# The product with v in two float32r halves, and an order of all instructions computed in the kernel

## The chip, the cores and the metric

The kernel runs on one core of a Trainium2 chip. The metric is the device time of one execution in microseconds (us), the median of several runs.

## The reference

Two requests (512 and 256 tokens, width 1024) go through the same two layers, in float32. Of a layer only the shape matters here; the change sits in the attentions, the three branches a, b and d:

```
h = rms_norm(x) * (1 + scale) + shift            # adaLN: scale, shift, gate from c
z = h @ w_in                                     # split into 14 parts
oa = MLA(4 heads, v of 64 columns)
ob = differential attention(4 heads, two softmaxes each, v of 64 columns)
oc = bidirectional RG-LRU
od = GQA(4 heads, 2 key heads, q and k normalised, v of 64 columns)
o  = concat(oa * silu(ga), ob * silu(gb), oc * silu(gc), od * silu(gd))
x  = x + gate * (o @ w_out)
```

An attention head is `p = softmax(q k^T * scale); o = p @ v`, over all keys of its own request.

## The kernel before, in words

**Numbers.** Most products run in float32r: each operand is split into a high part (rounded to float32r, written by ScalarE) and a low part (the rest, subtracted on VectorE or GpSimd), and `mm3` (L280 to L283) issues three matmuls, high by high, high by low, low by high. Where an operand is left in float32, one matmul does it; the profile shows such a matmul as two records on PE.

**Tokens.** Group 0 is the request of 512 tokens (four tiles of 128), group 1 the one of 256 (two tiles).

**An attention head** goes through three steps. The scores (L761 for b, L701 and L702 for d, `mm3` for a) go to PSUM buffers `s`, of which there are two. VectorE takes the extremes (L518, L520), ScalarE the exponential with its sum. In `transpose_pv` (L525) P is transposed tile by tile on PE (L535) into PSUM buffers `tr`, of which there are three, and copied to SBUF as `pt` by `copy(EN_E[...])`: key tiles 0, 1 and 3 of a head by ScalarE (L115), tile 2 by VectorE (L194). Then L542 multiplies v (float32, 64 columns) with P^T (float32, 512 or 256 columns). Even key tiles go to columns 0 to 63 of the array, odd ones to columns 64 to 127, so that two products can stand side by side; `o_evac` (L549) adds the two halves of the result. Over the 24 heads of the two layers and both groups that makes 96 products of 512 columns and 48 of 256. v comes from a projection as [tokens, 64 columns a head], copied by ScalarE in `v_evac` (L611), in tiles made by `v_tiles` (L604).

**What fills the gaps.** The other work of a layer (projections of the next branch, gates, adaLN chunks of 8 float32 matmuls with 32 columns at L227, weight splits) is written in between the heads' steps by `weave`, in a number per step that constants set (`F_D`, `F_A`, `F_B`, `LAG_*`). The recording layer's own scheduler then decides in what order the instructions stand on each engine. Buffers are named by a tag: `b` (47 of [128, 512]), `pt` (6), `p` (6), and so on. DMAs are issued by SP's queue in order; in branch b the stacks of q and k are put together by small DMAs (L747, L749).

**Stages of a layer**, with their times in the profiled execution for the first layer: projections to 92 us, branches d and a with the projections of a in between from 92 to 265, the LRU and the projections of b to 322, branch b to 437, the output projection after that. The second layer repeats them.

Of the kernel before, what the change touches and what calls it, by code (L numbers as in the profile page):

```python
# [18 lines left out]
P = 128  # L19
D = 1024  # L20
KC = 8
# [7 lines left out]
# order of the branches' chunks in the output projection  # L29
# [7 lines left out]
# steps of other work per job of a branch, by layer  # L37
# [6 lines left out]
# engines in turn: v DVE, g Pool, a ACT  # L44
# [8 lines left out]
EN_E, EN_V = ("aav", "a")  # L53
# [21 lines left out]
def body(ctx, tc, I, O, dbg=None):  # L75
# [5 lines left out]
    BUFS = {"ws": 4, "wh": 6, "wl": 6, "b": 47, "p": 6, "pt": 6, "rot": 2, "tmp": 2, "t1": 4}  # L81
# [19 lines left out]
    def gt(g, box, dt=F32R):  # L101
        """a [128, tokens of the group] tile; two of the small group share a slot, the second of them waiting in box"""
# [17 lines left out]
    # ---------------------------------------------------------------- constants  # L120
# [14 lines left out]
    # silu(c) in columns 0, 1 of a 32-column tile of the array, the others zero  # L135
# [13 lines left out]
    # rows 0..3 are rewritten, the others stay zero  # L149
# [5 lines left out]
    def rsqrt(v, n, tag="rs_y", bufs=3):  # L155
        """v ** -0.5 for a small tile [128, n]"""
# [58 lines left out]
    # ---------------------------------------------------------------- adaLN  # L215
# [5 lines left out]
    def ada_chunk(l, j, evac, deep):  # L221
        """512 columns: row 32 j + group is the partial sum over the chunks k = j (mod 4), in a column tile of its own"""
# [29 lines left out]
    def ada_gate(l):  # L252
        """gate rows of the two groups, to DRAM"""
# [15 lines left out]
    def load_split(src, n, kg, ncol, tl="wl", th="wh", eng="g"):  # L269
        """granules of kg contraction chunks x ncol columns, split into hi and lo"""  # L270
# [1033 lines left out]
```

## Time and profile before

| | |
|---|---|
| median of 3 runs | 966.57 us (966.34 to 968.16) |
| profiled execution | span 972.5 us; no time of its own is given beside the span |
| PE busy | 916.4 us |
| VectorE (DVE) busy | 667.2 us |
| ScalarE (ACT) busy | 546.6 us |
| GpSimd (POOL) busy | 148.8 us |
| granted TensorE clock, mean | 0.98 |

A busy PE is not PE at its peak: a matmul's record runs from its start to its modelled end, and the next one starts before that. The time that a matmul takes from the others is the step from its start to the start of the next, which the timeline shows.

### The profile page before, as it was taken

The numbers are of one execution on the slowest core, as the hardware profiler recorded it, in microseconds if no ns is written. First come the engines' busy times: TensorE is split into PE (matmuls) and PEld (weight loads), VectorE is DVE, ScalarE is ACT, GpSimd is POOL, SyncE is SP. The second block draws the span as 40 slices with busy tenths as digits, with TensorE's granted clock in tenths as the row PEclk, the third lists the DMA queues.
The fourth block names the chain that finished last, engine by engine and source line by source line (L and its number), as shares of the span: only waits on it lengthen the run. The fifth ranks groups of instructions, "written<-read, shape, count | busy, mean of one in ns | idle before, by whom it ended". The sixth has DMA issues, their size and how long they took to land.

```text
span 972.5 us, 15324 instructions
## 1 busy us (share of the span) xinstructions
PE 916.4 (94%) x5248; PEld 698.9 (72%) x5248; DVE 667.2 (69%) x1714; ACT 546.6 (56%) x1331; POOL 148.8 (15%) x168
## 2 busy tenths in 40 slices
PE   4899999999999799999999989999999899999996
PEld 1598767667989465676888976665689888666785
DVE  5687876655497656678556897676456786877745
ACT  4543878756545435466346367788447445667512
POOL 0221002003120010033202111000041212010610
PEclk9899999999999799999999999999999999999998
DMA  9731012123202633446611111020331114324502
GB/s 337 244 96 55 1 55 77 33 87 87 66 22 73 184 104 105 154 129 216 214 54 44 44 55 66 1 66 11 109 109 44 65 58 115 83 71 132 173 24 107
DMA packets 54350, 91.71 MB, mean 94 GB/s; under 512 B 9072, under 2 KB 13936, under 8 KB 54272
## 3 DMA queue, kind: packets, MB, share of 16 engines
q1 hardware_dynamic: 54272, 90.73, 30.1%
q8 instruction: 42, 0.69, 0.3%
q14 instruction: 36, 0.29, 0.1%
HBM read 73.38 MB, written 6.31 MB: 82 GB/s over the span
## 4 chain that ended last, share of the span: by engine, by line
PE 72%; DVE 13%; DMA 6%; issue 3%; ACT 3%; SPq 2%; POOL 1%; DVEq 0%; POOLq 0%; ACTq 0%
PE acc L281 10%; PE acc L283 10%; PE pv L542 10%; PE acc L282 9%; PE tr L535 5%; PE tr L281 4%; PE tr L282 3%; PE tr L283 3%; PE s L281 3%; PE s L282 3%; PE s L283 3%; DMA b<-ada 2%; PE acc L227 2%; PE tr L619 2%; PE s L761 2%
## 5 line engine op out<-in xcount | busy, mean ns | idle before, releaser
L212 POOL TENSOR_TENSOR wl<-ws,wh 128x512 fp32r<-128x512 f32 (+3 forms) x56 | 74.5, 1334 | 418.6 <-ACT wh L115 315.6
L115 ACT ACTIVATE p<-s,mx 128x512 f32<-128x512 f32 (+1 forms) x192 | 117.1, 615 | 30.6 <-DVE mx L518 27.5
L281 PE MATMUL acc<-wh,b 128*128 128x256 f32 (+4 forms) x360 | 113.0, 314 | 2.6 <-DVE rs_t L163 1.6
L282 PE MATMUL acc<-wl,b 128*128 128x256 f32 (+4 forms) x360 | 111.6, 310 | 0.0
L283 PE MATMUL acc<-wh,b 128*128 128x256 f32 (+4 forms) x360 | 111.2, 310 | 0.3 <-POOL b L318 0.3
L518 DVE TENSOR_REDUCE mx<-s 128x1 f32<-128x512 f32 x128 | 86.7, 686 | 27.8 <-PE s L761 17.6
L281 PE MATMUL acc<-b,wh 128*128 128x512 f32 (+1 forms) x288 | 103.3, 359 | 1.4 <-ACT wh L115 1.4
L542 PE MATMUL pv<-pt,b 128*64 128x512 f32 (+1 forms) x288 | 102.9, 546 | 1.4 <-ACT pt L115 1.0
L283 PE MATMUL acc<-b,wl 128*128 128x512 f32 (+1 forms) x288 | 102.0, 354 | 0.0
L282 PE MATMUL acc<-b,wh 128*128 128x512 f32 (+1 forms) x288 | 100.9, 350 | 0.0
L115 ACT ACTIVATE wh<-ws 128x512 fp32r<-128x512 f32 (+3 forms) x100 | 63.3, 639 | 41.4 <-PE tr L283 13.6
L535 PEld LDWEIGHTS tr<-c,p 128*128 128x128 f32 x480 | 55.2, 141 | 34.5 <-issue 17.9
L535 PE MATMUL tr<-c,p 128*128 128x128 f32 x480 | 75.9, 278 | 4.1 <-DVE b L864 2.2
L115 ACT ACTIVATE pt<-tr 128x512 f32<-128x512 f32 (+1 forms) x120 | 58.2, 511 | 35.2 <-PE tr L535 34.7
L281 PEld LDWEIGHTS acc<-wh,b 128*128 128x128 f32 (+1 forms) x360 | 68.8, 191 | 9.6 <-issue 2.4
L283 PEld LDWEIGHTS acc<-wh,b 128*128 128x128 f32 (+1 forms) x360 | 68.5, 191 | 6.9 <-issue 5.2
L282 PEld LDWEIGHTS acc<-wl,b 128*128 128x128 f32 (+1 forms) x360 | 69.2, 192 | 2.4 <-issue 0.8
L281 PEld LDWEIGHTS acc<-b,wh 128*128 128x128 f32 x288 | 55.0, 191 | 15.2 <-issue 5.2
L283 PEld LDWEIGHTS acc<-b,wl 128*128 128x128 f32 x288 | 54.8, 190 | 14.5 <-issue 7.8
L283 PE MATMUL tr<-wh,b 128*128 128x256 f32 (+2 forms) x216 | 62.1, 287 | 0.0
L281 PE MATMUL tr<-wh,b 128*128 128x256 f32 (+2 forms) x216 | 62.1, 287 | 0.0
L282 PE MATMUL tr<-wl,b 128*128 128x256 f32 (+2 forms) x216 | 62.0, 287 | 0.0
(306 smaller groups left out, 2201.5 us busy)
## 6 DMA issues: line engine op xcount, KB each, us to landing
ws<-wf SPq DMA_DIRECT2D x40, 256.0 KB, 3.2
b<-ada SPq DMA_DIRECT2D x32, 256.0 KB, 5.4
ws<-wt SPq DMA_DIRECT2D x32, 256.0 KB, 2.9
wh<-ada SPq DMA_DIRECT2D x32, 256.0 KB, 4.5
wl<-ada SPq DMA_DIRECT2D x32, 256.0 KB, 3.6
ws<-wo SPq DMA_DIRECT2D x32, 256.0 KB, 3.3
b<-b SPq DMA_DIRECT2D x112, 64.0 KB, 2.0
b<-b SPq DMA_DIRECT2D x112, 32.0 KB, 1.9
```

Source lines behind the costliest of these rows:

```text
L115: return nc.scalar.activation(out, in_, f, **kw)
L212: engine(eng).tensor_tensor(lo, w, hi.bitcast(F32), op=ALU.subtract)
L227: nc.tensor.matmul(acc[c:c + 32], cs[:, k], w, start=(k < 4), stop=(k >= 4))
L281: nc.tensor.matmul(out, sh, mh, start=first, stop=False)
L282: nc.tensor.matmul(out, sh, ml, start=False, stop=False)
L283: nc.tensor.matmul(out, sl, mh, start=False, stop=last)
L518: V.tensor_reduce(mx[:, i:i + 1], views[i], axis=AX.X, op=ALU.min)
L535: nc.tensor.transpose(tr[:, qt * P:(qt + 1) * P], Ps[qt // 2][:, qt % 2, kt * P:(kt + 1) * P], ident)
L542: nc.tensor.matmul(pv[64 * i:64 * i + 64, :n], vt[g][:, k0 + i], pts[i][:, :n], start=(k0 == 0), stop=(k0 + 2 == nk))
L619: nc.tensor.transpose(tr[:rows, i * P:(i + 1) * P], src(tt), ident)
L761: lambda out, qt: nc.tensor.matmul(out, q[:96, qt * P:(qt + 1) * P], k[:96], start=True, stop=True), g, h2, d) for (q, k), d in
```

## The change

It does four things.

1. **The product with v.** v is split into a high and a low float32r part, which lie side by side as 128 columns of the array: columns 0 to 63 high, 64 to 127 low. P^T is split too, by `split_evac`: ScalarE writes the high part, VectorE subtracts to get the low one. Each key tile now has two float32r matmuls, P^T low first and then P^T high, both over all 128 columns, so that the sum of the two halves that `o_evac` makes holds all four products. `EN_E` and `EN_V`, which chose the copying engine, are gone. The v tiles are twice as large.
2. **The order of products.** `mm3` issues the high by high product last instead of first, and the two-product scores of branch d the low keys first.
3. **The order of all instructions.** After the kernel is recorded, `arrange` goes through all of its instructions. It works out which depends on which, gives each a duration, and lists them as they would come ready: at each step the instruction that can start first on its engine, at equal times the one written first, with buffers handed out in the order in which the code asks for them. The list is then laid on the program as one chain of order without waits. The constants of `weave` stay.
4. **Buffers.** `b` has 51 instead of 47, `pt` 9 instead of 6; a smaller scratch area for DMA descriptors frees the room.

```diff
-    BUFS = {"ws": 4, "wh": 6, "wl": 6, "b": 47, "p": 6, "pt": 6, "rot": 2, "tmp": 2, "t1": 4}
+    BUFS = {"ws": 4, "wh": 6, "wl": 6, "b": 51, "p": 6, "pt": 9, "rot": 2, "tmp": 2, "t1": 4}
...
-    def mm3(out, sh, sl, mh, ml, first, last):
-        nc.tensor.matmul(out, sh, mh, start=first, stop=False)
-        nc.tensor.matmul(out, sh, ml, start=False, stop=False)
-        nc.tensor.matmul(out, sl, mh, start=False, stop=last)
+    def mm3(out, sh, sl, mh, ml, first, last, fresh="m"):
+
+        prods = [(sh, ml), (sl, mh), (sh, mh)]
+        if fresh == "s":
+            prods[:2] = prods[1::-1]
+        for i, (s, m) in enumerate(prods):
+            nc.tensor.matmul(out, s, m, start=first and i == 0, stop=last and i == 2)
...
-            for k0 in range(0, nk, 2):
-                pts = []
-                for kt in (k0, k0 + 1):
-                    tr = ps("tr")
-                    for qt in range(nk):
-                        nc.tensor.transpose(tr[:, qt * P:(qt + 1) * P],
-                                            Ps[qt // 2][:, qt % 2, kt * P:(kt + 1) * P], ident)
-                    pt = sb([P, 512], tag="pt")
-                    copy(EN_E[kt % len(EN_E)], pt[:, :n], tr[:, :n])
-                    pts.append(pt)
-                # even and odd key tiles in the two column tiles of the array, side by side
-                for i in range(2):
-                    nc.tensor.matmul(pv[64 * i:64 * i + 64, :n], vt[g][:, k0 + i], pts[i][:, :n],
-                                     start=(k0 == 0), stop=(k0 + 2 == nk))
-                yield
+            for kt in range(nk):
+                tr = ps("tr")
+                for qt in range(nk):
+                    nc.tensor.transpose(tr[:, qt * P:(qt + 1) * P], Ps[qt // 2][:, qt % 2, kt * P:(kt + 1) * P], ident)
+                ph, pl = (sb([P, 512], F32R, tag="pt") for _ in range(2))
+                split_evac(ph[:, :n], pl[:, :n], tr[:, :n])
+                for i, p in enumerate((pl, ph)):
+                    nc.tensor.matmul(pv[:, :n], vt(g, kt), p[:, :n], start=(kt == 0 and i == 0),
+                                     stop=(kt == nk - 1 and i == 1))
+                if kt % 2:
+                    yield
...
-            g, i0 = (0, tt) if tt < 4 else (1, tt - 4)
             for i, vt in enumerate(both):
-                copy(EN_V[i % len(EN_V)], vt[g][:, i0], src[:, P * i:P * i + P])
+                v = vt[tt // 2][:, tt % 2]
+                split_evac(v[:, :, 0], v[:, :, 1], src[:, P * i:P * i + P].rearrange("p (h d) -> p h d", h=2))
...
+    while len(order) < n:
+        best = None
+        for e, ks in ready.items():
+            for k in ks:
+                t0 = buffers(k)
+                if t0 is None:
+                    continue
+                s = max(came[k], t0)
+                key = (max(at[e], s + REACH[e] if s else 0.0), k)
+                if best is None or key < best:
+                    best = key
...
+    for a, b in zip(order, order[1:]):
+        tc.add_manual_dep(prog[b], prog[a].name,
+                          mybir.DependencyInfo(mybir.DependencyClass.NoSync, mybir.DependencyReason.DATA), reason="order")
...
     with tile.TileContext(nc) as tc:
         body(tc, I, O)
+        arrange(tc)
```

**Place 1, PE, first layer, the first head of branch d that reaches its product with v.** L535 are the transposes of P, L542 (L539 in the change) the products with v, L701 and L702 (L704 and L705) scores of a later head, `acc` with 320 columns the projection for branch a. Before:

```order
L535 MATMUL tr_1409<-c_83,p_1183 128x128 x2
L535 MATMUL tr_1409<-c_83,p_1292 128x128 x2
L701 MATMUL s_1500<-b_1139,b_1148 128x512
L702 MATMUL s_1500<-b_1140,b_1148 128x512
L542 MATMUL pv_1401<-pt_1407,b_576 64x512
L535 MATMUL tr_1418<-c_83,p_1183 128x128
L542 MATMUL pv_1401<-pt_1414,b_576 64x512
```

Now:

```order
L285 MATMUL acc_1547<-wh_1223,b_398 128x320
L285 MATMUL acc_1547<-wl_1231,b_445 128x320
L285 MATMUL acc_1547<-wh_1229,b_446 128x320
L285 MATMUL acc_1547<-wh_1229,b_445 128x320
L704 MATMUL s_1518<-b_1147,b_1155 128x512
L705 MATMUL s_1518<-b_1146,b_1155 128x512
L539 MATMUL pv_1408<-pt_1415,b_576 128x512
L539 MATMUL pv_1408<-pt_1414,b_576 128x512
L535 MATMUL tr_1431<-c_83,p_1190 128x128
L539 MATMUL pv_1408<-pt_1426,b_576 128x512
L539 MATMUL pv_1408<-pt_1425,b_576 128x512
```

Between the transposes of the first key tile and its product stood two score matmuls; now projection matmuls (four of six shown) stand there too, and the products are two per key tile, over 128 columns. The second product still has a single transpose between it and the first.

**Place 2, PE, first layer, the start of branch b.** L761 (L764) are the scores of b, L227 (L226) a chunk of adaLN, `acc` with 512 columns a gate's projection. Before:

```order
L761 MATMUL s_3972<-b_3866,b_3865 128x512
L761 MATMUL s_3973<-b_3866,b_3865 128x512
L761 MATMUL s_3986<-b_3858,b_3857 128x512
L761 MATMUL s_3987<-b_3858,b_3857 128x512
L761 MATMUL s_3997<-b_3866,b_3865 128x512
L761 MATMUL s_3998<-b_3866,b_3865 128x512
L761 MATMUL s_4119<-b_3944,b_3943 128x512
L761 MATMUL s_4120<-b_3944,b_3943 128x512
L281 MATMUL acc_4054<-b_365,wh_4044 128x512
```

Now:

```order
L764 MATMUL s_4153<-b_4047,b_4046 128x512
L285 MATMUL acc_4235<-b_377,wh_4225 128x512
L285 MATMUL acc_4235<-b_376,wh_4225 128x512
L285 MATMUL acc_4235<-b_387,wl_4227 128x512
L764 MATMUL s_4154<-b_4047,b_4046 128x512
L285 MATMUL acc_4235<-b_388,wh_4225 128x512
L285 MATMUL acc_4235<-b_387,wh_4225 128x512
L285 MATMUL acc_4235<-b_398,wl_4227 128x512
L285 MATMUL acc_4235<-b_399,wh_4225 128x512
L764 MATMUL s_4167<-b_4039,b_4038 128x512
```

Eight scores stood in a row there, with nothing between; now three or four matmuls of a gate's projection stand between each two.

**Place 3, VectorE, the same head as in place 1.** L518 (L520) are extremes of scores, L200 scales P, rows of 128x2 belong to a norm of the projection. Before:

```order
L194 COPY pt_1423<-tr_1418 128x512
L200 TENSOR_SCALAR t_354_1373<-pt_1350,rsq_1361 128x128
L593 RECIPROCAL den_1498<-den_1498 128x2
L518 TENSOR_REDUCE mx_1513<-s_1515 128x1
L200 TENSOR_SCALAR p_1496<-p_1496,den_1498 128x512
```

Now:

```order
L460 TENSOR_TENSOR pt_1415<-tr_1409,pt_1414 128x512
L164 SCALAR_TENSOR_TENSOR rsq_1368<-rs_t_1370,rsq_1368 128x2
L162 SCALAR_TENSOR_TENSOR rs_t_1370<-rsq_1368 128x2
L460 TENSOR_TENSOR pt_1426<-tr_1420,pt_1425 128x512
L163 TENSOR_TENSOR rs_t_1370<-rs_t_1370,rs_v_1364 128x2
L591 RECIPROCAL den_1394<-den_1394 128x2
L520 TENSOR_REDUCE mx_1516<-s_1518 128x1
```

One key tile of the four was copied by VectorE (this is it); now VectorE subtracts for each of the four (two are shown), behind ScalarE's copy.

## Rows read from the trace of the kernel before

**Rows 1.** The page: span, busy time by engine, chain that ended last.

```profile
span 972.5 us, 15324 instructions
PE 916.4 (94%) x5248; PEld 698.9 (72%) x5248; DVE 667.2 (69%) x1714; ACT 546.6 (56%) x1331; POOL 148.8 (15%) x168
PE 72%; DVE 13%; DMA 6%; issue 3%; ACT 3%; SPq 2%; POOL 1%; DVEq 0%; POOLq 0%; ACTq 0%
```

**Rows 2.** Groups by form, PE: xcount | busy us, mean ns | idle before.

```profile
L542 PE MATMUL pv<-pt,b 128*64 128x512 f32 x192 | 82.6, 617 | 0.3 <-DVE pt L194 0.2
L542 PE MATMUL pv<-pt,b 128*64 128x256 f32 x96 | 20.4, 405 | 1.2 <-ACT pt L115 1.0
```

**Rows 3.** Timeline of PE around products with v: start us, us, what.

```profile
112.04 1.07 PE L542 MATMUL pv<-pt,b 128*64 128x512 f32 x2
113.04 0.33 PE L535 MATMUL tr<-c,p 128*128 128x128 f32 x1
...
124.36 1.83 PE L542 MATMUL pv<-pt,b 128*64 128x512 f32 x4
126.12 0.33 PE L535 MATMUL tr<-c,p 128*128 128x128 f32 x1
...
198.22 1.08 PE L542 MATMUL pv<-pt,b 128*64 128x512 f32 x4
199.22 0.39 PE L282 MATMUL tr<-b,kvh 128*128 128x256 f32 x1
...
229.64 0.65 PE L542 MATMUL pv<-pt,b 128*64 128x256 f32 x4
230.22 0.27 PE L237 MATMUL tr<-c,tmp 128*128 128x2 f32 x1
```

**Rows 4.** Timeline of PE in projections in float32r.

```profile
300.05 0.28 PE L281 MATMUL acc<-wh,b 128*128 128x256 f32 x1
300.17 0.28 PE L282 MATMUL acc<-wl,b 128*128 128x256 f32 x1
...
476.31 0.39 PE L281 MATMUL tr<-b,b 128*128 128x512 f32 x1
476.54 0.40 PE L282 MATMUL tr<-b,b 128*128 128x512 f32 x1
```

**Rows 5.** Groups by form, DVE and ACT, of evacuations from PSUM.

```profile
L194 DVE COPY pt<-tr 128x512 f32<-128x512 f32 x24 | 16.5, 688 | 16.9 <-PE tr L535 16.9
L458 DVE TENSOR_TENSOR b<-tr,b 128x512 fp32r<-128x512 f32 x4 | 2.7, 681 | 0.0
L458 DVE TENSOR_TENSOR b<-tr,b 128x256 fp32r<-128x256 f32 x4 | 1.6, 411 | 0.0
L639 DVE TENSOR_TENSOR t<-acc,pt 128x128 f32<-128x128 f32 x4 | 1.1, 278 | 0.0
L115 ACT ACTIVATE pt<-tr 128x512 f32<-128x512 f32 x72 | 42.0, 596 | 27.7 <-PE tr L535 27.4
```

**Rows 6.** Windows: stretch, its length, busy us of each engine, granted clock, DMA.

```profile
92.00:265.00 173.00, 172.02 (x992) 124.99 (x991) 110.32 (x294) 120.47 (x322) 22.16 (x39) 1.00 0.19 57
324.00:342.40 18.40, 13.39 (x33) 4.92 (x32) 12.66 (x22) 9.76 (x25) 1.31 (x1) 0.63 0.57 165
328.70:342.40 13.70, 9.95 (x16) 3.98 (x17) 9.32 (x16) 6.91 (x18) 1.31 (x1) 0.50 0.64 191
809.00:897.00 88.00, 85.73 (x455) 60.77 (x453) 68.57 (x146) 58.39 (x156) 7.71 (x6) 1.00 0.36 100
```

**Rows 7.** Waits of PE and its weight loads: us in total, times, longest.

```profile
PE acc L227 <- DVE rs_t L179: 13.2, 1, 13.2
PEld pv L542 <- ACT pt L115: 19.4, 45, 0.9
PEld s L761 <- ACT p L115: 13.5, 22, 1.9
PE tr L281 <- DVE rot L194: 6.0, 2, 3.0
```

More of the change, by code (lines that the diff above doesn't have):

```diff
@@ L52 @@
 EN_L = "g"
-EN_E, EN_V = ("aav", "a")
 ADA_T = ("wh", "wl") * 4
@@ L450, in feat_tile @@
                 for k in range(KC):
-                    mm3(acc[:, :n], his[k // 4][:, k % 4], los[k // 4][:, k % 4], hh[k], hl[k], k == 0, k == KC - 1)
+                    mm3(acc[:, :n], his[k // 4][:, k % 4], los[k // 4][:, k % 4], hh[k], hl[k], k == 0, k == KC - 1, "s")
                 evac(g, t0, n, acc)
@@ L700, in scores @@
                 s = q[:, qt * P:(qt + 1) * P]
-                nc.tensor.matmul(out, s, kh, start=True, stop=False)
-                nc.tensor.matmul(out, s, kl, start=False, stop=True)
+                nc.tensor.matmul(out, s, kl, start=True, stop=False)
+                nc.tensor.matmul(out, s, kh, start=False, stop=True)
             def attn():
@@ L1187, in body, with _accesses @@
         H = Hn
+def _accesses(aps):
+    for a in aps:
+        ap = getattr(a, "bass_ap", None)
+        t = getattr(ap, "tensor", None)
+        if t is None or not hasattr(t, "cap_key"):
+            continue
+        if t._space == bass.MemoryType.DRAM:
+            offs = np.array([ap.offset // 512])
+            for s, c in ap.ap:
+                offs = (offs[:, None] + s * np.arange(0, c, 1 if s >= 512 else 512) // 512).ravel()
+            p0, pn = 0, 1
+        else:
+            width = int(np.prod(t.shape[1:]))
+            p0, f0 = divmod(ap.offset, width)
+            pn = ap.ap[0][1]
+            offs = np.array([f0])
+            for s, c in ap.ap[1:]:
+                offs = (offs[:, None] + s * np.arange(c)).ravel()
+        mask = 0
+        for o in set(offs.tolist()):
+            mask |= 1 << o
+        yield t, p0, p0 + pn, mask
@@ new lines, in _cost @@
+def _cost(i):
+    kind, eng = type(i).__name__, i.engine
+    size = lambda a: int(np.prod([c for _, c in a.ap[1:]]))
+    outs = [a for a in i.outs if hasattr(a, "ap")]
+    ins = [a for a in i.ins if hasattr(a, "ap")]
+    n = max([size(a) for a in outs + ins] or [1])
+    if kind == "InstMatmult":
+        n, cols, f32 = size(i.ins[0]), size(i.ins[1]), i.ins[0].dtype == F32
+        if not f32:
+            return max(n * 0.44 + 4, 115), n / 2.4 + 172
+        if cols <= 64 and n > 128:
+            return n / 1.2 + 30, n / 0.6 + 160
+        if n == 128:
+            return 110, 273
+        return (215, 362) if n < 128 else (n / 0.6 + 8, n / 0.6 + 170)
+    if eng == mybir.EngineType.SP:
+        return (590 if outs[0].ap[0][1] == 32 else 375), n * 4 * outs[0].ap[0][1] / 230.0
+    psum = any(a.bass_ap.tensor._space == bass.MemoryType.PSUM for a in outs + ins if size(a) > 4)
+    if eng == mybir.EngineType.Activation:
+        s = 0.84 * n + (50 if psum else 92)
+        if i.func not in (AF.Copy, AF.Square):
+            s += 110
+        if len(outs) > 1:
+            s += 90
+        return s, s + 100
+    if eng == mybir.EngineType.Pool:
+        return 2.3 * n + 90, 2.3 * n + 135
+    if kind in ("InstTensorScalarPtr", "InstTensorCopy") and not psum and len([a for a in ins if size(a) == n]) == 1:
+        s = 0.66 * n + 70
+    else:
+        s = 1.04 * n + 65
+    return s, s + 80
@@ L1294 @@
     arrays = _layout(inputs)
-    nc = bacc.Bacc("TRN2", target_bir_lowering=False, num_devices=1)
+    nc = bacc.Bacc("TRN2", target_bir_lowering=False, num_devices=1, dynamic_dma_scratch_size=512)
     I = {n: nc.dram_tensor(n, a.shape, mybir.dt.from_np(a.dtype), kind="ExternalInput").ap()
```

110 lines of the change are left out of this document (107 added, 3 removed).

## The prediction

> **What bounds the kernel now.** I read the page first: PE is busy 916.4 us of a span of 972.5, VectorE 667, ScalarE 547, and 72% of the chain that ended last runs over PE [rows 1]. So time is won where PE needs fewer steps, or where it waits. Then the groups of PE by form: the products with v, 288 records of L542, are busy 82.6 + 20.4 us [rows 2]. Then the timeline around them, for the step from one start to the next, because a busy PE is not a full one: a product of 512 columns that stands alone keeps PE for 1.00 us (112.04 to 113.04); two that are issued close together take 1.00 for both; but two whose second comes late take 1.76 [rows 3]. Last the windows and waits: in branches d and a PE is busy 172 of 173 us, yet at the start of branch b it idles 5 of 18.4 us, and for 13.7 us of it the granted clock is 0.50, the 1.2 GHz level, after scores that waited for exponentials [rows 6, 7].
>
> **The products with v.** Their rows take 103.0 us of PE [rows 2]. The last record of each stretch runs 0.07 into what follows (1.07 against a step of 1.00, [rows 3]); with at most 144 stretches that is 10 at most, so PE loses 93 to 103 us to them. I take 97, since many stand in pairs. The change issues 2 x 96 float32r matmuls of 512 columns and 2 x 48 of 256, all over 128 columns. The trace shows no float32r product with v; the nearest rows are projections, which step by 0.23 us at 512 columns and 0.12 at 256 [rows 4]: 192 x 0.23 + 96 x 0.12 = 56. **Gain 41 us**, at most 47. At least 6: had all 48 pairs of 512 columns and 24 of 256 been close, they would cost 48 x 1.00 + 24 x 0.58 = 62 [rows 3].
>
> That low end is also what a rule gives. The Trainium skill, TensorEngine Tiling (Array Packing), section Tiling Modes, says under Key Properties that tiles operate independently, so that different tiles can run their matmuls in parallel. By that rule the pair was cheap already, and the sum below would end at 957 instead of 922. The close pair in this trace (1.00 us for two) agrees; the single and the staggered ones (1.00 each, 1.76 for two) show that the kernel mostly didn't get it, because the second P^T landed late: 45 waits for ScalarE's copy, 19.4 us [rows 7].
>
> **The start of branch b.** Eight scores stood in a row, each waiting for an exponential to free one of two PSUM buffers, and the order now has three or four projection matmuls between them (place 2). That work is moved from later, where PE is the bound, so what is won is PE's idle time and its slow clock. Idle: 18.4 - 13.4 = 5.0 us. The clock: 13.7 us at half speed with PE busy 9.95 [rows 6], of which full speed could save up to half, 5. **Gain 10 us.** At least 3, if the stacks' DMAs, still 24 issues in one queue, hold the scores up and the clock still falls; at most 17, where the next stretch profits too (the waits of L761 are 13.5 in all, [rows 7]).
>
> **The rest of the order.** Elsewhere the two orders stand close to each other: at the other stage borders PE still meets the same chains. The transposes of the LRU's end wait for VectorE's `rot` twice, 6.0 us, and the first matmul waits 13.2 [rows 7]; both stay. In the middle some waits for operands go. **Gain 4 us**: 56 us of PE idle in all [rows 1], less 13.2, 5 and 6 leave 32, of which I credit an eighth, as the order is much the same there; bounds 25 gained and 5 lost (an order from wrong durations makes an engine wait in line for something that is not there yet). High by high as the last product of `mm3` costs nothing in count: three steps of 0.12 or 0.23 as before [rows 4], one weight load each; but a group now starts with a low part, which lands last, so a late split stalls it one product earlier. That lies in the same bounds.
>
> **What VectorE and ScalarE pay.** VectorE subtracts the low part of 96 P^T tiles of 512 columns at 0.681, 48 of 256 at 0.411, and of 60 tiles of v at 0.278, and no longer copies 24 tiles at 0.688 [rows 5]: 65.4 + 19.7 + 16.7 - 16.5 = **+85 us**, 667 to 752. ScalarE gets 24 copies more, 24 x 0.596 = 14. No DMA is added, and GpSimd keeps its work. What hides it: PE's own work, while it has some. In d and a VectorE is busy 110 of 173 us; the share that falls there is 26 a layer (d and a: 16 x 0.681 + 8 x 0.411 - 4 x 0.688 = 11.4 each; v 3 tiles a token tile, 18 x 0.278 = 5, less what falls in the projections), so 136 of some 160: covered. In branch b of the second layer it is busy 68.6 of 88 [rows 6] and gets 11 more, while PE needs 7 less there: 80 of 81. There it is the bound, and PE's gain is mostly not to be had: 5 us. At the ends of the six branches no other work covers the last head; the product then waits for copy and subtraction in turn, one 0.68 longer: 6 x 0.68 = 4. **Cost 10 us with the borders of the projections**; below, 2 if all but the ends is covered; above, 30 if a third of the 85 shows. Three more `pt` buffers hold 4.5 key tiles in two parts each, against six tiles before; `tr` is held 0.68 longer per tile, three buffers as before. Both lie in that upper bound.
>
> **Sum.** 972.5 - 41 - 10 - 4 + 10 = 927.5 us of span. The profiled execution has no time of its own beside its span, which is 5.9 above the median of 966.6; the same 5.9 off gives **922 us**.
>
> **The rivals.**
>
> *The evacuation becomes the bound (0.16).* If VectorE can't keep up in the attentions, PE's 41 us turn into waits of L539 for VectorE, and only the order's 14 us are left: 972.5 - 14 - 5.9 = 953. For it: 80 of 81 in the second layer's branch b. Against it: 136 of 160 in d and a, and projections between transposes and products now (place 1). The Trainium skill has this as a rule, TensorEngine Tiling (Array Packing), section PSUM Bottleneck: speeding up PE doesn't speed up the evacuation of PSUM, which may become the bottleneck. No row here shows it yet.
>
> *The products gain only 6 us (0.05).* The lower end above: the new products step by 0.3 us on average instead of 0.2, as each waits for a semaphore and stands between float32 transposes. Then 972.5 - 6 - 10 - 4 + 10 - 5.9 = 957, the time of the rule on tiles too. Against it: projections with waits keep their steps [rows 4].
>
> *The order closes more (0.15).* Upper ends of the gains, 47 + 17 + 25, and 5 of cost: 972.5 - 84 - 5.9 = 883. For it: VectorE and ScalarE have 31% and 44% to spare over the span. Against it: the borders look the same in both orders.
>
> *Slower (0.06).* Each key tile's transposes need one of three `tr` buffers, which now stays taken until VectorE has subtracted. If VectorE is late, as it serves extremes of scores (0.68 each) from the same queue, PE can't transpose and can't multiply, and in order nothing behind them runs. Then the subtractions themselves, 65.4 + 19.7 = 85 us, lie on the path. The gains are 41 + 10 + 4 = 55; so the kernel gets slower once more than two thirds of the 85 show, and with all of it 972.5 - 55 + 85 - 5.9 = 997. Against it: PE's other work in d and a.
>
> *It doesn't move (0.04).* The order loses what the product wins, in waits by wrong durations: 967.
>
> **How the numbers follow.** Forecast 0.54, the rivals as given. The range takes in the forecast with its bounds, most of the better case and the evacuation bound: 885 to 953. It leaves out the slower case, no change, the 957, and a third of the better case, 0.06 + 0.04 + 0.05 + 0.05. A measurement can tell 0.2%, 1.9 us. Faster by more than that: 0.54 + 0.16 + 0.05 + 0.15 = 0.90; within it 0.04; slower 0.06.
>
> **What would show it.** Right: the products are 288 float32r matmuls that step by 0.23 or 0.12 (their rows, each some 0.17 longer than its step, would show about 80 busy us instead of 103); VectorE rises to about 750 and ScalarE to 560; the window of branch b's start keeps the clock at 1.00; PE's waits at the LRU's end stay. The first rival shows as waits of L539 for L460 of tens of us; the slower case as waits of L535 for L460. Wrong would be: products that step by much more than 0.23, or new stretches at half clock in the attentions.

## The result, and the profile after

The change is slower: 974.28 us, median of 6 runs (972.48 to 976.09), against 967.37 (6 runs, 965.13 to 970.68) of the kernel before beside it; ratio 1.0076, 95% interval 1.0051 to 1.0100. The forecast was 922 us in 885 to 953. The profiled execution is the one of 972.48 us, 1.8 above its span.

The page of the changed kernel, against [rows 1]:

```profile
span 970.7 us, 15498 instructions
PE 890.3 (92%) x5248; PEld 721.7 (74%) x5248; DVE 734.7 (76%) x1894; ACT 559.4 (58%) x1355; POOL 152.3 (16%) x168
PE 47%; DVE 32%; ACT 11%; issue 4%; DMA 3%; SPq 2%; POOL 1%; DVEq 0%; ACTq 0%; POOLq 0%
```

TensorE (PE) is busy 26 us less, and the span has hardly moved: PE idles 80 us instead of 56. VectorE (DVE) is busy 68 us more, and its share of the chain that ended last went from 13% to 32%. The products came as announced in number and form. PE's groups by form, then its timeline around them, against [rows 2, 3]:

```profile
L539 PE MATMUL pv<-pt,b 128*128 128x512 f32 x192 | 67.7, 434 | 5.6 <-DVE pt L460 4.9 <-DVE b L549 0.3
L539 PE MATMUL pv<-pt,b 128*128 128x256 f32 x96 | 21.7, 321 | 4.1 <-DVE pt L460 2.5 <-DVE b L549 1.3
```

```profile
111.67 0.73 PE L539 MATMUL pv<-pt,b 128*128 128x512 f32 x2
112.24 0.92 PE L535 MATMUL tr<-c,p 128*128 128x128 f32 x7
...
114.45 1.32 PE L539 MATMUL pv<-pt,b 128*128 128x512 f32 x4
115.61 0.27 PE L856 MATMUL tr<-c,pt 128*96 128x128 f32 x1
```

Two of 512 columns take 0.57 us to the next start, four 1.16: 0.29 each, where two float32 ones took 1.00 for a pair, and the 0.23 of the projections is not quite reached. Over all 192 in this trace the step is 0.28 on average and 0.24 in the median; all 288 records step by 70.9 us together, against 96.6 in the trace before. VectorE pays what was counted: its groups by form, against [rows 5]. All its groups together take 82.5 us more; the page's busy time counts records that overlap once, and rises by 68.

```profile
L460 DVE TENSOR_TENSOR pt<-tr,pt 128x512 fp32r<-128x512 f32 x96 | 64.8, 682 | 3.2 <-ACT pt L114 2.7
L460 DVE TENSOR_TENSOR pt<-tr,pt 128x256 fp32r<-128x256 f32 x48 | 19.5, 416 | 5.3 <-ACT pt L114 5.1
```

The same windows as in [rows 6], with two more stretches at half clock (columns as there):

```profile
92.00:265.00 173.00, 165.63 (x973) 130.22 (x972) 132.40 (x356) 122.58 (x325) 22.78 (x39) 0.99 0.19 54
324.00:342.40 18.40, 16.07 (x77) 11.99 (x76) 9.84 (x19) 7.32 (x19) 1.28 (x1) 0.81 0.58 160
809.00:897.00 88.00, 80.10 (x435) 61.41 (x434) 81.23 (x170) 63.10 (x166) 8.81 (x7) 1.00 0.35 101
408.40:415.20 6.80, 5.04 (x12) 2.95 (x13) 5.10 (x13) 2.59 (x10) 0.00 (x0) 0.50 0.42 125
442.60:449.40 6.80, 6.80 (x22) 5.83 (x23) 6.34 (x14) 5.22 (x14) 1.19 (x2) 0.50 0.69 223
```

In branches d and a of the first layer PE is idle 7.4 us where it was 1.0, with VectorE at 132 of 173. The start of branch b got better, as forecast: PE idles 2.3 of 18.4 us instead of 5.0, and the granted clock is 0.81 there instead of 0.63. But later in that branch two stretches of 6.8 us at 0.50 (the 1.2 GHz level) are new, and others elsewhere are gone: over the whole execution 42.0 us lie at that level, in the first trace of the kernel before 41.6. In the second layer's branch b VectorE is busy 81 of 88 us. Waits, against [rows 7] (us in total, times, longest):

```profile
PEld pv L539 <- DVE pt L460: 25.0, 62, 1.5
PEld s L764 <- ACT p L114: 14.4, 26, 3.1
...
PE acc L262 <- DVE tmp L260: 6.5, 2, 4.9
PE tr L236 <- DVE tmp L233: 4.7, 5, 1.5
...
ACT p L114 <- DVE mx L520: 43.5, 38, 4.5
```

The last line is ScalarE's exponentials waiting for VectorE's extremes of the scores; in the trace before it was 27.5 us:

```profile
ACT p L115 <- DVE mx L518: 27.5, 31, 2.3
```

### The profile page after: what moved, and what is told of

It reads as the page before. It is cut to its first block, busy times and chain, and to the rows that moved or that the text cites. A ratio compares the mean times of both kernels' runs of the same rounds, so it can differ in the third digit from the quotient of the medians.

```text
span 970.7 us, 15498 instructions
## 1 busy us (share of the span) xinstructions
PE 890.3 (92%) x5248; PEld 721.7 (74%) x5248; DVE 734.7 (76%) x1894; ACT 559.4 (58%) x1355; POOL 152.3 (16%) x168
## 3 DMA queue, kind: packets, MB, share of 16 engines
q1 hardware_dynamic: 54272, 90.73, 30.4%
## 4 chain that ended last, share of the span: by engine, by line
PE 47%; DVE 32%; ACT 11%; issue 4%; DMA 3%; SPq 2%; POOL 1%; DVEq 0%; ACTq 0%; POOLq 0%
PE acc L285 20%; PE tr L285 10%; PE s L285 7%; ACT p L114 5%; DVE mx L520 4%; DVE pt L460 3%; PE pv L539 3%; DVE p L770 2%; ACT b L114 2%; PE tr L535 2%; PE acc L226 2%; DVE b L460 2%; ACT tmp L114 1%; DVE b L463 1%; DVE b L549 1%
## 5 line engine op out<-in xcount | busy, mean ns | idle before, releaser
L285 PE MATMUL acc<-wh,b 128*128 128x256 f32 (+4 forms) x720 | 161.1, 311 | 0.0
L285 PE MATMUL acc<-b,wh 128*128 128x512 f32 (+1 forms) x576 | 155.8, 351 | 0.0
L285 PEld LDWEIGHTS acc<-b,wh 128*128 128x128 f32 x576 | 101.5, 191 | 13.2
L539 PE MATMUL pv<-pt,b 128*128 128x512 f32 (+1 forms) x288 | 89.4, 396 | 9.7 <-DVE pt L460 7.4
L520 DVE TENSOR_REDUCE mx<-s 128x1 f32<-128x512 f32 x128 | 86.3, 682 | 12.3 <-PE s L764 11.7
L460 DVE TENSOR_TENSOR pt<-tr,pt 128x512 fp32r<-128x512 f32 (+1 forms) x144 | 84.3, 593 | 8.5 <-ACT pt L114 7.8
L535 PE MATMUL tr<-c,p 128*128 128x128 f32 x480 | 78.2, 279 | 7.4 <-DVE p L770 3.5
L114 ACT ACTIVATE pt<-tr 128x512 fp32r<-128x512 f32 (+1 forms) x144 | 74.4, 525 | 17.7 <-PE tr L535 17.4
L285 PE MATMUL tr<-wh,b 128*128 128x256 f32 (+2 forms) x432 | 81.3, 287 | 0.0
L535 PEld LDWEIGHTS tr<-c,p 128*128 128x128 f32 x480 | 57.9, 142 | 27.6 <-DVE p L770 6.7
L539 PEld LDWEIGHTS pv<-pt,b 128*128 128x128 f32 x288 | 45.6, 190 | 36.6 <-DVE pt L460 25.0
L285 PEld LDWEIGHTS tr<-wh,b 128*128 128x128 f32 x432 | 67.3, 188 | 0.7
L114 ACT ACTIVATE b<-tr 128x128 fp32r<-128x128 f32 (+7 forms) x92 | 39.9, 448 | 38.9 <-PE tr L622 10.5
```

The costliest lines, as they stand in the source:

```text
L114: return nc.scalar.activation(out, in_, f, **kw)
L285: nc.tensor.matmul(out, s, m, start=first and i == 0, stop=last and i == 2)
L460: V.tensor_tensor(lo, src, hi.bitcast(F32), op=ALU.subtract)
L520: V.tensor_reduce(mx[:, i:i + 1], views[i], axis=AX.X, op=ALU.min)
L535: nc.tensor.transpose(tr[:, qt * P:(qt + 1) * P], Ps[qt // 2][:, qt % 2, kt * P:(kt + 1) * P], ident)
L539: nc.tensor.matmul(pv[:, :n], vt(g, kt), p[:, :n], start=(kt == 0 and i == 0), stop=(kt == nk - 1 and i == 1))
```

## The experiments

Two theories at first: **V** (W in the texts of the first three runs), that VectorE's new subtractions take back what the products give; and **O**, that the change's own order loses it. Every run was timed beside the kernel before on its chip, so ratios are compared, and a hundredth of ratio is 9.7 us. The clock is the median of the mean granted clocks of a kernel's runs: with levels of 0.5 and 1.0, a mean of 0.975 is 5% of the time at 1.2 GHz.

| kernel | us | ratio to before (95%) | clock |
|---|---|---|---|
| before again (e4) | 970.2 | 1.0009 (0.9986–1.0032) | 0.985 |
| the change | 974.3 | 1.0076 (1.0051–1.0100) | 0.979 |
| without its own order (e1) | 973.1 | 1.0033 (1.0008–1.0058) | 0.969 |
| before + own order alone (e2) | 994.5 | 1.0258 (1.0228–1.0289) | 0.987 |
| change, no subtraction (e3) | 959.5 | 0.9896 (0.9868–0.9924) | 0.985 |
| e1, no subtraction (e5) | 941.7 | 0.9731 (0.9695–0.9767) | 0.983 |
| e1, old order of products (e6) | 965.4 | 0.9971 (0.9949–0.9993) | 0.975 |
| change, old order of products (e7) | 970.6 | 1.0030 (1.0007–1.0052) | 0.984 |
| change, half of P's scaling on GpSimd (e8) | 979.6 | 1.0115 (1.0066–1.0164) | 0.978 |
| e6, all of P's scaling on ScalarE (e9) | 966.9 | 0.9955 (0.9936–0.9973) | 0.975 |
| e6, weights' low parts on GpSimd (e10) | 974.0 | 1.0044 (1.0028–1.0060) | 0.967 |
| e6, no subtraction (e11) | 940.5 | 0.9686 (0.9669–0.9702) | 0.987 |
| e6, subtraction made, not read (e12) | 965.7 | 0.9984 (0.9960–1.0008) | 0.972 |
| e6, products in pairs (e13) | 970.5 | 1.0019 (1.0001–1.0038) | 0.970 |
| e11 + dead VectorE work (e14) | 965.1 | 0.9961 (0.9939–0.9984) | 0.974 |
| before + dead VectorE work (e15) | 991.9 | 1.0234 (1.0188–1.0280) | 0.977 |
| split in d and a only (e16) | 962.8 | 0.9954 (0.9934–0.9974) | 0.983 |
| e16, scaling on ScalarE (e17) | 962.6 | 0.9942 (0.9922–0.9961) | 0.981 |

### The parts apart: e1, e2, e3, and before again, e4

```diff
 # e1: the change without arrange     # e2: the kernel before with it
-        arrange(tc)
```

```diff
 # e3: the change; both products of a key tile read the high part
-                split_evac(ph[:, :n], pl[:, :n], tr[:, :n])
-                for i, p in enumerate((pl, ph)):
+                act(ph[:, :n], tr[:, :n])
+                for i, p in enumerate((ph, ph)):
```

The low part of P^T is then missing and the high part counts twice; the work of TensorE is the same.

> The change without its own order of instructions: products, splits and buffers as changed, the order left to the recording layer's scheduler. Theory W (VectorE's subtractions stand in front of the products and take back what PE wins): as slow as the change, 968 to 980 us. Theory O (the new order loses what the products win): 925 to 945 us.

> The kernel before with the new order alone: float32 products with v, old copies, old order of products in mm3. Theory W: 950 to 968 us, the order is neutral or gains my 14 us. Theory O: 985 to 1010 us.

> The change, but VectorE doesn't subtract the low part of P^T: both products of a key tile read the high part (the output lacks the low part). PE issues as many matmuls as in the change; VectorE has 144 subtractions less, 84 us. Theory W: 920 to 940 us. Theory O: 965 to 975 us.

> The kernel before once more, for a second profile: its first profiled execution, span 972.5 us, was longer than its runs. Expected by both: 965 to 968 us, a span of some 965, the start of branch b without 13.7 us at half clock. If the span is 972 again, a profiled execution of it is simply longer.

The new products in the framework's order (that of the recording layer's scheduler) gain nothing (1.0033). The own order alone, on the float32 products, costs 2.6%, 25 us. And the subtraction costs the change 1.8%, 17 us; e3's 959.5 us fell between the two ranges. So both theories held a part. e4 missed its 965 to 968 us: 970.2, with a profiled span of 969.9 (1.8 under its own time) and 10.2 us at half clock at the start of branch b, where the first trace has 13.7. What remains without subtraction and own order, e5 asks.

### Neither subtraction nor own order: e5

> The framework's order (as in the run without the arranged order, 973.1 us) with no subtraction of P^T's low part: both products of a key tile read the high part, so the low part is missing and the high part counts twice in the output. VectorE loses the same 65 us as in the arranged kernel without the subtraction (959.5 us). Theory V (VectorE's work in the heads' chains is what holds the attentions, and the order is indifferent): 957 to 961 us, PE busy about 875. Theory O (the arranged order loses some 15 us that VectorE's lateness hides as long as the subtraction is there): 940 to 948 us. If it stays above 968, the subtraction costs only in the arranged order, since that order puts it in front of something urgent.

0.9731, the figure of theory O: without the subtraction the own order costs 0.9896 - 0.9731 = 1.65%, 16 us, and the subtraction costs the framework's order 3.0%, 29 us. Two waits go with the own order, in each of the change, e2, e3 and e7, against before, e1, e5 and e6. Here in the change without subtraction (e3), then in its pair in the framework's order (e5):

```profile
PE acc L262 <- DVE tmp L260: 7.8, 3, 5.5
PE tr L236 <- DVE tmp L233: 4.3, 4, 2.3
...
ACT p L114 <- DVE mx L520: 41.1, 37, 4.9
```

```profile
PE tr L236 <- DVE tmp L233: 0.4, 1, 0.4
...
ACT p L114 <- DVE mx L520: 23.4, 30, 2.0
```

In the four PE waits 7 to 12 us in line for VectorE's evacuations of the modulation's chunks (L260, L233), at most 1.1 in the others, and the exponentials wait 41 to 45 us for VectorE, 11 to 18 more than in each one's pair. Of the 18.7 us by which e3's span is longer than e5's, 11.3 lie in branches d and a, from the first to the last product with v of each layer (116.4 to 121.9 and 113.3 to 119.1 us). Which of the own order's durations is wrong, and whether these waits are the whole cost, wasn't tried.

### The order of the products: e6, e7

```diff
-        prods = [(sh, ml), (sl, mh), (sh, mh)]
-        if fresh == "s":
-            prods[:2] = prods[1::-1]
+        prods = [(sh, mh), (sh, ml), (sl, mh)]
...
-                nc.tensor.matmul(out, s, kl, start=True, stop=False)
-                nc.tensor.matmul(out, s, kh, start=False, stop=True)
+                nc.tensor.matmul(out, s, kh, start=True, stop=False)
+                nc.tensor.matmul(out, s, kl, start=False, stop=True)
```

e6 is this edit in e1, e7 in the change.

> The framework's order, the split products with v, but the three products of a split matmul and the two of a score in their old order (high by high first). Theory V: the order within a group changes nothing that VectorE does, so 971 to 975 us like the kernel that differs only in this. Theory M (a group that begins with a low part stalls PE until the late split has landed, which is part of the +7 us of waits of other matmuls): 964 to 969 us, and PE's waits for VectorE in front of L281's and L285's products shrink by some 5 us.

> The change with its own order of all instructions, but the three products of a split matmul and the two of a score in their old order. Theory V: 972 to 976 us. Theory M: 966 to 970 us, as in the pair without the arranged order. If this one moves and the other doesn't, the products' order matters only through where the arranged order puts the splits.

High by high first is faster by 0.6% in the one and by 0.46% in the other, 4 to 6 us; the kernel with the split products and nothing else (e6) is 0.3% faster than before. The times come near theory M's ranges, but not its sign: PE's waits for VectorE in front of `mm3`'s products should have shrunk by some 5 us, and they shrank by 3.0 in e6 (13.2 to 10.2) and 0.3 in e7 (7.1 to 6.8). In e6 the mean clock is 0.975 and in e1 0.969, which is 12 us less at the 1.2 GHz level; half of that would be the 6 us. So how it gains is not shown.

### VectorE's work given to others: e8, e9, e10

```diff
 # e8, in the change
-EN_P, EN_D, EN_M = ("va", "vv", "va")
+EN_P, EN_D, EN_M = ("ga", "vv", "va")
 # e9, in e6
-EN_P, EN_D, EN_M = ("va", "vv", "va")
+EN_P, EN_D, EN_M = ("aa", "vv", "va")
 # e10, in e6
-EN_T, EN_F, EN_W, EN_A = ("gvv", "gggv", "ggv", "gv")
+EN_T, EN_F, EN_W, EN_A = ("g", "g", "g", "gv")
```

> The change, with the half of P's scaling that VectorE did (48 operations) given to GpSimd, which is busy 152 of 971 us: VectorE falls by about 21 us to some 714. Theory V (the subtraction's 65 us cost 15, so 0.23 us for each us of VectorE): 968 to 971 us if GpSimd is no slower in the chain than VectorE was; with a GpSimd operation two or three times as long as VectorE's 0.43, each lies in a head's chain from score to transpose and the time is 974 to 985 us. A rival, that PE and the order set the time and VectorE doesn't: 974 us whatever GpSimd takes.

> The split products with v alone (framework's order, old order of products: 965.4 us), with the half of P's scaling that VectorE did (48 operations, 22.0 us) given to ScalarE, which does the other half. Theory V (VectorE holds the attentions; without the subtraction's 65 us the framework's order gained 31, so 0.48 us for each us of VectorE): about 955 us, with ScalarE's busy time up by some 25 us. A rival, that the head's chain counts and not VectorE's load: the two scalings of a pair now stand one behind the other on ScalarE, between exponentials, and the time stays within 964 to 968 or grows.

> The split products with v alone (965.4 us), with the low parts of the weights, of which VectorE does 44 in 38 us, all given to GpSimd (1.4 us each there, some 60 us more of an engine that is busy 152). Theory V, if VectorE's load counts wherever it lies: up to 0.48 x 38 = 18 us less, 947; but most of these 44 lie in the projections, where VectorE has room, so only what falls in the attentions counts: 958 to 964. The rival, that weights become late on GpSimd: 968 or more, with PE's waits for wl.

None gains. GpSimd's group of scalings in e8, then VectorE's in e6:

```profile
L199 POOL TENSOR_SCALAR p<-p,den 128x512 f32<-128x512 f32 (+1 forms) x48 | 65.2, 1358 | 146.9 <-DVE den L591 131.1 <-ACT pt L114 9.3 <-DVE rs_t L162 2.4
```

```profile
L199 DVE TENSOR_SCALAR p<-p,den 128x512 f32<-128x512 f32 (+1 forms) x48 | 22.0, 459 | 0.4
```

One takes three times as long there (1358 ns against 459), in the head's own chain: 1.0115 against the change's 1.0076, with intervals that overlap (from 1.0066 and up to 1.0100), in the range expected of a slow GpSimd. On ScalarE (e9) the ratio goes from 0.9971 to 0.9955, inside the intervals, where theory V's simple price would have given 10 us: VectorE's spared 22.0 us of scalings are ScalarE's added 23 (559.3 to 582.6) in the same chain of score, extreme, exponential, scaling, transpose. Giving the weights' low parts to GpSimd (e10) is slower by 0.7%, and the clock is down to 0.967. The sign that was named for it is missing: PE's weight loads wait 1.7 us for these parts from GpSimd, 1.4 in e6. So in e9 less work for VectorE gained nothing while ScalarE, in the same chain, took it over; why e10 is slower, with VectorE busy 16 us less, isn't shown.

### Load, buffer, or wait: e11, e12, e14, e13

Four kernels are to tell by what way the subtraction costs. All are e6 with another body of the loop over key tiles. In the first three both products read the high part, as in e3.

```diff
 # e11: no subtraction
+                act(ph[:, :n], tr[:, :n])
 # e12: subtraction from PSUM as in e6, not read
+                split_evac(ph[:, :n], pl[:, :n], tr[:, :n])
 # e14: a subtraction out of SBUF, not read
+                act(ph[:, :n], tr[:, :n])
+                V.tensor_tensor(pl[:, :n], ph[:, :n].bitcast(F32), ph[:, :n].bitcast(F32), op=ALU.subtract)
 # e13: e6 whole, the products of two key tiles after the transposes of both
+                for i in range(2):
+                    for kt in (k0, k0 + 1):
+                        nc.tensor.matmul(pv[:, :n], vt(g, kt), pts[kt - k0][i][:, :n], start=(kt == 0 and i == 0),
+                                         stop=(kt == nk - 1 and i == 1))
```

> The split products with v alone and no subtraction of P^T's low part: both products of a key tile read the high part, so the low part is missing and the high part counts twice in the output. It is the kernel before with its products with v replaced and VectorE's load nearly as before (some 20 us more of o's and v's work). Theory V: the product itself is worth 26 to 41 us (PE's steps for it fell from 97 to 68 in the split kernel), of which the subtraction eats all but a few: 930 to 941 us. If the old order of the products still gains its 7 us here, 935; if VectorE's relief and the old order overlap, 941 as with the new order.

> The split products with v alone (965.4 us), with VectorE's subtraction still made from the PSUM buffer, but its result read by nobody: both products of a key tile read the high part, so the low part is missing and the high part counts twice in the output. VectorE's load and the time for which the PSUM buffer is held are those of the 965.4 us kernel; what is gone is that the product waits for the subtraction. Theory L (latency: PE's low product waits in line for the subtraction): 940 to 946 us, nearly as without it. Theory V (VectorE's load, or the buffer held for it): 960 to 966 us. Between them the shares of the two can be read off.

> As the kernel without the subtraction (940.5 us; high part read twice, low part missing), but VectorE makes a subtraction of the same size out of SBUF alone (high part minus itself), which nobody reads: it holds no PSUM buffer and no product waits for it. Theory V in its plain form (the load delays VectorE's other work, such as extremes of scores): 960 to 966 us. If only the held PSUM buffer or the product's wait costs: 940 to 944 us.

> The split products with v alone (965.4 us), with the products of two key tiles issued after the transposes of both, high parts first, as the kernel before had its pairs: nothing is added or left out. Theory L: the low products come about 1 us later, so the subtraction's latency is hidden: 946 to 958 us. Theory V: VectorE's load is the same, 962 to 968 us.

The answer is clear: 0.9686 without the work, 0.9961 with dead work (nobody reads its result) that holds no PSUM buffer, 0.9984 with the buffer held too, 0.9971 with all of it. **VectorE's load alone brings the price**: 2.75 of 2.85 hundredths, each with some 0.3 of uncertainty, 27 us for 89 us of work. One rival is left by the edit: the dead work also takes a second `pt` buffer per key tile and reads the first. In e14's trace no copy of ScalarE waits for it, and PE's weight loads wait for it once, for 0.8 us.

The wait of the low product, which the profile shows so plainly (25.0 us of PE's weight loads in the change), is worth nothing that can be measured. One reason is in the lines: where no product waits for the subtraction, the products' weight loads wait as long for ScalarE's copy. Here e6, e12, and e11 without any subtraction:

```profile
PEld pv L537 <- DVE pt L458: 17.0, 27, 1.9
```

```profile
PEld pv L537 <- ACT pt L114: 23.1, 51, 1.3
```

```profile
PEld pv L537 <- ACT pt L114: 19.9, 56, 2.5
```

Issuing the products in pairs (e13) left 2.9 us of the wait for the subtraction and 18.3 for the copies, and made the kernel slower (970.5, above both ranges), not faster. Busy times of e11, then of e14, on their pages, and VectorE's dead group in e14:

```profile
PE 874.3 (93%) x5248; PEld 717.2 (76%) x5248; DVE 663.7 (71%) x1750; ACT 558.0 (59%) x1355; POOL 149.3 (16%) x168
```

```profile
PE 885.8 (92%) x5248; PEld 722.8 (75%) x5248; DVE 729.6 (76%) x1894; ACT 558.6 (58%) x1355; POOL 155.2 (16%) x168
```

```profile
L536 DVE TENSOR_TENSOR pt<-pt 128x512 fp32r<-128x512 f32 (+1 forms) x144 | 88.9, 624 | 5.5 <-ACT pt L114 4.5
```

PE's same 5248 matmuls are busy 11.5 us longer, and it idles 11 us longer (64.6 and 75.3 of the span). The clock could explain some 9 of the 11.5, an estimate: half of the 18.7 us that e14's profiled execution spends more at the 1.2 GHz level (45.5 and 26.8). The exponentials' waits for the extremes rise from 27.6 us in e11 to 36.1 in e14:

```profile
ACT p L114 <- DVE mx L518: 27.6, 30, 2.4
```

```profile
ACT p L114 <- DVE mx L518: 36.1, 38, 3.5
```

### The same load in the kernel before: e15

```diff
                     copy(EN_E[kt % len(EN_E)], pt[:, :n], tr[:, :n])
+                    z = sb([P, 1], tag="z", bufs=4)
+                    V.tensor_reduce(z, pt[:, :n], axis=AX.X, op=ALU.min)
```

> The kernel before (967 us, VectorE busy 667) with one reduction by VectorE more per key tile of P^T, 144 in all and some 85 us, out of SBUF, read by nobody. Theory V, that VectorE stands right behind TensorE as the second bound, so that its load costs once TensorE's products are cheap: in the kernel before TensorE still covers much of it, 968 to 980 us. If VectorE's load costs the same 0.3 us for each us whatever TensorE does: some 992 us, and then the faster products and the dearer VectorE are two separate terms that happen to cancel.

1.0234: 23 us for VectorE's dead 82.8, although TensorE's products are the old ones. It's the second of the two expectations: VectorE did not become a bound by the faster products; its work was on the path all along, at 0.27 us for each us, near e14's 0.30. (By the page's busy time, which rises by 58 us here and 66 in e14, both are some 0.4.) The trace of e15 has no wait for the dead reductions. Branches d and a of the first layer, from the last rope of the first projections to the LRU, in windows of before again (e4) and of e15, and the exponentials' waits in both:

```profile
86.00:237.00 151.00, 148.37 (x811) 101.84 (x812) 102.41 (x301) 108.87 (x294) 16.52 (x31) 1.00 0.18 56
```

```profile
85.00:246.00 161.00, 153.56 (x820) 106.28 (x821) 124.12 (x354) 109.98 (x296) 16.82 (x32) 0.97 0.18 53
```

```profile
ACT p L115 <- DVE mx L518: 28.2, 31, 2.2
```

```profile
ACT p L115 <- DVE mx L518: 48.3, 44, 3.0
```

VectorE is at 102 of 151 us before and at 124 of 161 with the load: it has room in the mean, and the stretch is still 10 us longer, in nearly the same work (811 and 820 matmuls). PE waits 7.4 us of it instead of 2.6, and the clock fell. As I read it, the load delays what VectorE does next, the extremes wait in its queue, the exponentials wait for them, and PE stands in line behind scores and transposes: over the whole execution PE's waits of the scores L761 (L763) for exponentials go from 4.1 to 6.8 us, its weight loads' waits of the transposes for ScalarE's copies from 1.7 to 9.1.

### A version that beats both: e16, e17

e16 is e6 with the float32 pairs of the kernel before kept in branch b; in d and a the split. e17 also gives all of P's scaling to ScalarE.

```diff
 # transpose_pv takes the old loop when it is given the old v tiles
+            if isinstance(vt, list):
...
+                done(pv)
+                return
 # diff(), branch b
-            both, Vs = v_tiles(4)
+            both, Vs = v_tiles_old(4)
...
-                v_evac(both, tt, acc)
+                v_evac_old(both, tt, acc)
```

> The split products with v alone (965.4 us), but only in branches d and a; branch b keeps the float32 pairs of the kernel before, with its copies by ScalarE and VectorE in turn. VectorE's work in branch b falls by some 25 us for the two layers, TensorE's rises by some 12. Theory V: branch b's stretches (228.7 us with the split in the profile, 225.2 before) come back to before, and the time is 960 to 964 us. If the split pays in branch b too: 968 to 972.

> As the run with the split products in branches d and a only, and with ScalarE doing all of P's scaling there (VectorE 22 us less, all of it in d and a, ScalarE some 25 more). Theory V: 955 to 962 us. The rival, that ScalarE's place in the head's chain takes back what VectorE is spared, as in the run with that move alone (966.9): the same as the kernel with the split in d and a only, within 2 us.

0.9954 and 0.9942 (0.9922 to 0.9961): 4 and 6 us faster than before, 12 and 13 faster than the change. e16's 962.8 is in theory V's range, but against e6 (0.9971), which beats both kernels too, neither step stands clear of the intervals by itself. e17 isn't the 955 to 962 of theory V but the rival's case.

## Why the prediction was wrong

The forecast was 45 us under the median (-41 - 10 - 4 + 10); the measurement is 7.4 above it. Kernels in a row split that (ratios times 967.4):

| step | kernels | predicted | measured | time at 1.2 GHz, us |
|---|---|---|---|---|
| products with v | before to e11 | -41 | -30.4 ± 1.6 | 29 to 24 |
| subtraction, by VectorE | e11 to e6 | +10 | +27.6 ± 2.7 | 24 to 48 |
| low parts first | e6 to e1 | 0 | +6 ± 3 | 48 to 60 |
| own order | e1 to the change | -14 | +4 ± 3 | 60 to 42 |

The first step holds the new buffers too, and v's subtractions, which the copies that VectorE no longer makes pay for (its page has 667.2 and 663.7). The last three steps depend on the way taken. By e11, e5, e3 and the change, low parts first come out at +4, the own order at +16 and the subtraction at +17. On either way two steps of the prediction failed: VectorE's work, called mostly covered, and the order, which was to gain. They are off by 18 us each in the table, by 7 and 30 on the other way.

- **The products: right in mechanism, mis-sized.** 288 float32r matmuls, as said; in e11 PE is busy 42 us less than in the kernel before (874.3 and 916.4), and 30 of 41 reach the end. Their steps fell by 34 us in the traces (96.6 as counted, to 62.9 in e11, where 56 was forecast): most step by 0.23 and 0.12, but the mean is 0.26 and 0.14. That projections with waits keep their steps was no reading of [rows 4], which show no wait. The rival of 6 us, with the Trainium skill's rule that tiles run in parallel (TensorEngine Tiling (Array Packing), section Tiling Modes), is out as a forecast: the close pairs did agree with it (1.00 us for two), but most products weren't close pairs. Of the 64 stretches of products of 512 columns in the trace before, 33 hold a single one, and of the 30 pairs 7 take 1.1 us or less.
- **VectorE's 85 us: this step failed.** The prediction counted 85 and called the cost 10, since "136 of 160" in d and a was "covered". The 85 was right in the attentions (84.3 us for P^T), and its price was 27.6 in the framework's order, near the upper bound of 30 that "a third of the 85" had set, and 17 in the change's own. Filling 85% of a stretch was not cover here, where the engine serves a chain through three engines: e15 shows that the kernel before, with VectorE at 68% of that stretch, pays much the same. The 81 of 88 in the second layer's branch b came as forecast, but it was d and a that paid: from the first to the last product with v, e6 is longer than e11 by 9.6 and 8.8 us there in the two layers, by 0.4 and 2.6 in branch b.
- **The rivals.** The evacuation as the bound (953) came nearest in kind, and its sign, tens of us of L539 waiting for L460, is there with 25.0 us. But e12 and e14 show that this wait isn't the price. The rule behind it, PSUM Bottleneck in the Trainium skill's TensorEngine Tiling (Array Packing), speaks of tiling that speeds up TensorE and not the evacuation. It isn't what these runs show: e14's dead work doesn't touch PSUM, and costs as much. The slower rival, `tr` held for the subtraction, has the right side for a wrong reason: its sign, L535 waiting for L460, isn't in the change's trace, and e12 holds the buffer where e14 doesn't, 0.9984 and 0.9961, with intervals that overlap. Its turning point, two thirds of the 85 shown, wasn't needed either: a third was enough, as the order lost instead of gaining.
- **The start of branch b: right in place, given back.** PE's idle time there fell by 2.7 us and the time at half clock from 13.7 to 6.8, about 6 us of the 10, or 5 against e4, which idles 5.6 us there and has 10.2 at half clock. New half-clock stretches later in the branch (rows above) are what the text named as wrong.
- **The rest of the order: this step failed too, wrong in sign.** It was to gain 4, between 25 gained and 5 lost, as "the two orders stand close to each other" outside b's start. With b's start in it the own order costs 4 us with the subtraction (6 by e6 and e7), 16 without (e3, e5), 25 with the float32 products (e2). The text had named the way, an engine that waits in line for what isn't there yet; the 7 to 12 us of PE's waits for the modulation's chunks and the 11 to 18 more of the exponentials' fit it. Why the three differ is not settled; the first starts from the lowest clock (e1 at 0.969, e5 and before at 0.983 and 0.985), which the own order brought back, the others had little to win there.
- **Low parts first: costed at nothing,** with "a late split stalls it one product earlier" in the bounds. It costs 4 to 6 us; the waits that went with it are 3.0 and 0.3 us, so by what way isn't shown.
- **The offset.** The 5.9 us between the first profiled span and the median was one long execution (e4's span is 1.8 under its own time); it cancels out of the differences.

How much of these terms goes with the clock can be estimated. If each us at 1.2 GHz loses half a us, the subtraction's 24 more are 12 of its 27.6, the low parts' 12 are their whole 6, and the own order, which brings 18 back, gains 9 by them and loses 13 elsewhere. Half is near what the runs show: a straight line through the ten runs of e1 rises by 0.57 us for each us at the lower level, one through the 25 of before beside e12 by 0.39. The clock may fall because PE waits, so these need not be separate causes; how much would remain with the clock held wasn't tried.

## What to carry over

Before work moves from TensorE to another engine, measure that engine's price with dead work of the same size in the old kernel: one run (e15) would have told 23 us where the busy shares told 10. A wait that a profile names need not be worth its length, and an engine that was 68% busy in a chain of three engines had no free room here. Test a new order of instructions by itself, with each form of the kernel that it is meant for; here it cost 4, 16 or 25 us, depending on what else was late.

## What was not expected of the hardware

In these kernels small differences in PE's work went with the granted clock, and by the estimate above with a good part of the cost. In e1, at the end of the second layer's branch b, the window before is at 1.00 and the next 17.1 us at 0.50; e11 keeps 1.00 in the same place (windows of e1, then of e11, as above):

```profile
853.50:870.70 17.20, 15.68 (x103) 13.37 (x102) 15.48 (x34) 12.16 (x37) 0.00 (x0) 1.00 0.13 32
870.70:887.80 17.10, 13.59 (x45) 9.08 (x44) 11.70 (x40) 7.83 (x27) 0.00 (x0) 0.50 0.51 169
```

```profile
829.00:846.20 17.20, 16.19 (x98) 13.39 (x97) 11.70 (x24) 12.00 (x33) 3.00 (x2) 1.00 0.29 89
846.20:863.30 17.10, 15.53 (x96) 11.79 (x95) 14.70 (x43) 13.21 (x42) 0.00 (x0) 1.00 0.48 152
```

What PE did before it fell in e1, in its timeline: a wait for an exponential, and eight transposes of two columns each, which had just begun.

```profile
869.07 0.51 PE L764 MATMUL s<-b 96*128 96x256 f32 x2 [1.51 <-ACT p L114]
869.41 0.90 PE L539 MATMUL pv<-pt,b 128*128 128x256 f32 x4
870.32 1.58 PE L810 MATMUL tr<-c,tmp 128*128 128x2 f32 x8
```

VectorE is busy 15.48 of the 17.2 us before the fall, 11.70 in e11's window. Which of these made the clock fall isn't shown: e11's second window has PE busy about as long as e1's first (15.53 and 15.68 us) and stays at 1.00. From 24 to 64 us of a run lie at the lower level in these kernels (means of 0.987 and 0.967).
